# Thirteen experts sorted by load, none fixed at the end, and one light list treated apart in the ending

## The chip, the cores and the metric

The kernel runs on one core of one Trainium2 chip. A core has a matmul engine (PE, with its weight loads PEld), a vector engine (DVE), an activation engine (ACT), a general engine (POOL), a sync engine (SP) that only issues transfers here, and 16 DMA engines. The metric is the device time of one execution in microseconds (us); less is better. A profile is one further execution, recorded by the hardware profiler.

## The reference, cut to what matters

One block of a network over 512 tokens of width 1024: a token mixer, and after it a mixture of 16 experts in which every token goes to 2 experts. Only the second half is touched by the change.

```
h2 = modulate(rmsnorm(x, g_pre_ffn), shift2, scale2)
x = x + gate2 * rmsnorm(hier_moe(h2), g_post_ffn)

hier_moe: g_sel = argmax(h @ w_router_group); top 2 of the 4 experts of that group
  for e in range(16):
    a = silu(h @ w_gate[e]) * (h @ w_up[e])          # 1024 -> 512
    y = y + combine[:, e, None] * (a @ w_down[e])    # 512 -> 1024
```

All is float32. The weights of one expert are 3 x 2 MB, those of all experts 96 MB; they are read once from HBM.

## The kernel before, in words

**Lists.** After the router the kernel makes, for each expert, a list of the tokens that chose it, in slots of 128, 64 or 32 rows. Positions are numbered by `c`. Three experts are static (`c` 0 to 2, 128 slots). Eleven (`NDYN`, `c` 3 to 13) are sorted by load on the chip, heaviest first: the first `NHV` = 5 ranks have 128 slots, the next `NL64` = 3 have 64, the last three 32. The weights of a sorted expert are loaded from an address in a register of SP. Two more experts (`c` 14 and 15) are fixed, with 128 slots each. `c` = 16 (`NE`) is an extra list of 32 slots for the tokens of the heaviest expert beyond 128. If any list is longer than its slots, a loop at the end (`tc.If(novf > 0)`) does the rest with a second pass over the output.

**Positions.** `SEQ` gives the order in which the experts are worked off, one `position` each: `gate_up` (eight blocks of 512 KB, gate and up in turn, four parts of two) and `down` (four blocks of 512 KB), `down` one position late. A list of 128 slots is heavy: ACT and DVE split each weight block into a high and a low part (lines 1328 and 1329), and PE makes three products. A list of 64 or 32 slots is light: PE takes the blocks as they are (tiles `gul` and `yl`), in 2 or 4 groups of rows. The blocks go through a ring of 25 buffers in SBUF; SP issues the loads in program order (line 1306).

**Output.** `down` scales its product by the router's weight (ACT, line 1556 for a light list, 1559 and 1560 for a heavy one), and POOL adds the rows to `ybuf` in HBM by an indirect transfer (line 1580). The rows of `h2` are fetched by POOL as well (line 1335).

**Ending.** `setup` runs in the last position: SP loads the last blocks early, then a broadcast row `g2` and the rows `x1` (lines 1825, 1829), and POOL loads the four tiles `ys` of `ybuf` (line 1832). `scale` takes each tile's norm: a square sum on ACT (1845), a small operation on DVE (1840), a power on POOL (1841), a product on DVE (1847), and a product with `rest` on POOL (1850), the share of the tile's tokens that the ending does not treat apart. `write` makes the output tile on DVE (1854) and SP stores it (1855). `after(engine, ...)` chains an instruction behind the last one of its engine. The two fixed experts are treated apart: their rows are gathered from `ybuf` before their product is in it (1815), `last` adds the product and takes the norm per row, `put` scales them, and an indirect transfer adds them to the output (1872), one expert after the other.

**Small numbers for the routing.** `R(...)` takes columns of a small buffer; `ohr` is the one-hot matrix of the sort (`NDYN` x `NDYN`), and `rest` is made from `Ab`, which says who chose which expert. `psA` is a pool of four PSUM banks, from which the output projection before the experts takes its tiles `y`: four for its left half, then again four for its right half (line 1221 and following, helpers `wout_mm`, `half`).

Of the kernel before, what the change touches and what calls it, by code (L numbers as in the profile page):

```python
# [21 lines left out]
EPS = 1e-6  # L22
# [3 lines left out]
NE, DE = 16, 512  # L26
NOV = 13

NPRE, NDYN = 3, 11

NHV, NL64 = 5, 3
STAR = NPRE

SEQ = [0, 1, 2, 11, 3, 8, 4, 12, 5, 9, 6, 13, 7, 10, 14, 15]


def groups_of(c):

    r = c - NPRE
    return 4 if c == NE else 1 if r < NHV or r >= NDYN else 2 if r < NHV + NL64 else 4  # L40

def expert_at(p):

    return 4 * (p % 4) + p // 4

NA1, NA2, LOW, NRAW, NHL = 10, 5, 100, 25, 5
# [130 lines left out]
def body(ctx, tc, I, C, out, dbg=None):  # L179
# [1236 lines left out]
    def indices(x0_, x1_, src):  # L1416
        return V.scalar_tensor_tensor(iiv[:, x0_:x1_], src[:, :, 0], OOB, src[:, :, 1], op0=OP.add, op1=OP.add)
# [231 lines left out]
    with tc.issue_after(listed.ins):  # L1649
# [4 lines left out]
        ohr, t3 = R(NDYN, NDYN), R(NDYN, 3, NDYN)  # L1654
# [41 lines left out]
        indices(NPRE + NDYN, NE, ls[:, NPRE + NDYN:NE, :])  # L1696
        for c in range(NPRE + NDYN, NE):
            lsr[c] = ls[:, c, :]

        NLT = NDYN - NHV  # L1700
        lst2, ix = R(NLT + 1, 3), R(NLT + 1)
# [44 lines left out]
    parts_sum(l4v[:, 1:4, :, 1], lqv[:, :, 32:80].rearrange("p q (e c) -> p q e c", c=3))  # L1746
    G.tensor_scalar(l4v[:, :, :, 0].bitcast(I32), lof, OOB, None, op0=OP.add)

    rest = R(4)
    V.tensor_tensor(rest, Ab[:, :, NE - 2], Ab[:, :, NE - 1], op=OP.add)  # L1750
    V.tensor_scalar(rest, rest, -1.0, 1.0, op0=OP.mult, op1=OP.add)
    run["upto"] = len(seq)
    for e in range(1, NPRE):
        position(e, static_w(e))
# [103 lines left out]
    def last(i):  # L1858
        yg, w, c = fin["yg"][i], lists_of(LAST[i])[1], 24 + 4 * i
        for n in range(2):  # L1860
            s = slice(n * 512, n * 512 + 512)
            after(V, lambda: V.scalar_tensor_tensor(yg[:, s], py[i][n], w, yg[:, s], op0=OP.mult, op1=OP.add))
            after(S, lambda: S.activation(fin["junk"][:, s], yg[:, s], AF.Square, accum_out=st[:, c + 3 * n:c + 3 * n + 1]))
        after(V, lambda: V.tensor_tensor(st[:, c:c + 1], st[:, c:c + 1], st[:, c + 3:c + 4], op=OP.add))
        inv(c)
        after(V, lambda: V.tensor_tensor(yg.ap, yg.ap, fin["G2"], op=OP.mult))

    def put(i):
        zg, r = fin["yg"][i], st[:, 25 + 4 * i:26 + 4 * i]
        after(S, lambda: S.mul(zg[:, 0:512], zg[:, 0:512], r))  # L1870
        after(V, lambda: V.tensor_scalar(zg[:, 512:1024], zg[:, 512:1024], r, None, op0=OP.mult))
        after(G, lambda: G.indirect_dma_start(out=outv, out_offset=bass.IndirectOffsetOnAxis(ap=iiv[:, LAST[i]:LAST[i] + 1], axis=0),
                                              in_=zg.ap, in_offset=None, bounds_check=T - 1, oob_is_err=False, compute_op=OP.add))


    def last_products(raws):
        sg = run["pend"][2][0][0]
        tp = pT("at")
        for q in range(4):
            PE.transpose(tp[:, q * 128:(q + 1) * 128], sg[:, q * 128:(q + 1) * 128], ident)  # L1880
        after(S, lambda: S.copy(sg.ap, tp))
        y = pA("y0"), pA("y1")
        for kk in range(4):
            for n in range(2):
                mm(y[n], sg[:, kk * 128:kk * 128 + 128], raws[kk][:, n * 512:n * 512 + 512], kk == 0, kk == 3)
        py.append(y)

    py = []

    def first():  # L1890
        py.append(run["py"])
        for tt in range(2):
            scale(tt, True)

    run.update(setup=lambda: setup(True), first=first)
    for n in range(NPRE, NE):
        c = SEQ[n]
        if c >= NPRE + NDYN:
            position(n, static_w(c))
        else:  # L1900
            position(n, dyn_w(nc.values_load(idi[0:1, c:c + 1], engines=(mybir.EngineType.SP,), min_val=0, max_val=NE - 1)))
    raws = [raw_unit(run["pend"][1], 2, kk) for kk in range(4)]
    line.update({V: run["mul"], S: run["silu"]})
# [9 lines left out]
    for i in range(2):  # L1913
        for n in range(2):
            s = slice(n * 512, n * 512 + 512)
            after(S, lambda: S.mul(yob[i][:, s], py[i][n], lists_of(LAST[i])[1]))
# [47 lines left out]
```

## Time and profile before

| | |
|---|---|
| Runs shown | 640.63, 642.20, 642.83 us; median 642.2 |
| Profiled execution | 641.7 us, of which 639.9 us is the span from first to last instruction |
| PE, DVE, ACT, POOL busy | 86%, 58%, 46%, 34% of the span |
| PE clock granted, mean | 0.949 of 2.4 GHz |
| DMA, mean | 265 GB/s, 169.43 MB |

The span is what the rows below tell of; 1.8 us lie around it. A share of busy time is a mean over stages with different limits, so each claim is read from its own stage.

### The profile page before, as it was taken

To read this page: it belongs to the slowest core of one execution; us is meant where nothing else is said; L and a number is where in the kernel's file an instruction comes from. 1 tells how busy PE (TensorE), PEld (TensorE's weight loads), DVE (VectorE), ACT (ScalarE), POOL (GpSimd) and SP (SyncE) were. 2 spreads that over 40 slices of the span, in tenths; PEclk is the share of its full clock that TensorE was granted. 3 is DMA by queue.
4 is the path that set the end of the run, shared out by engine and by line. 5 is a ranking of instruction groups with operands and counts; after the bars stand their busy time and mean duration, and the time that the engine had idled before them with its cause. 6 is when DMAs were issued, how large, how long until landed. Compare 5 with 4: busy or idle time off the path is not lost.

```text
span 639.9 us, 9115 instructions
## 1 busy us (share of the span) xinstructions
PE 548.7 (86%) x3065; PEld 379.3 (59%) x3065; DVE 368.1 (58%) x689; ACT 294.5 (46%) x478; POOL 218.4 (34%) x264
## 2 busy tenths in 40 slices
PE   3779979699999869998679899999999989988940
PEld 1256955688665547875568676657654647355610
DVE  3560693826237663427978997753653527165781
ACT  2560626443125335224258684653744545165722
POOL 8343850066124345617440317312211010002152
PEclk9979998899999988999599999999999999999985
DMA  9975601121599794247689799999999999999631
GB/s 266 389 257 190 239 0 33 50 82 66 174 321 311 263 352 165 67 163 270 239 340 357 254 350 398 335 369 381 387 383 391 384 387 390 390 404 372 263 134 24
DMA packets 59542, 169.43 MB, mean 265 GB/s; under 512 B 9433, under 2 KB 16885, under 8 KB 59492
## 3 DMA queue, kind: packets, MB, share of 16 engines
q1 hardware_dynamic: 50820, 156.17, 65.4%
q0 software_dynamic: 6112, 12.18, 7.4%
q10 hardware_dynamic: 2560, 0.47, 0.5%
q8 instruction: 25, 0.41, 0.3%
q14 instruction: 25, 0.20, 0.1%
HBM read 157.02 MB, written 17.12 MB: 272 GB/s over the span
## 4 chain that ended last, share of the span: by engine, by line
PE 52%; DMA 19%; DVE 12%; issue 6%; POOL 6%; ACT 4%; POOLq 0%; ACTq 0%; DVEq 0%; SPq 0%
PE y L211 9%; DMA U<-in_w_gate_dram 9%; PE gate L211 6%; PE up L211 6%; PE gul L211 4%; PE uz L211 3%; DMA U<-in_w_ada_dram 3%; PE yl L211 2%; PE win L211 2%; PE ada2p L839 2%; PE num L211 2%; DMA U<-in_w_down_dram 2%; PE xe L211 1%; DVE U L489 1%; PE ada1p L211 1%
## 5 line engine op out<-in xcount | busy, mean ns | idle before, releaser
L1329 DVE TENSOR_TENSOR U<-U,U 128x1024 fp32r<-128x1024 f32 x114 | 135.5, 1232 | 42.7 <-ACT U L1328 42.2
L1328 ACT CAST U<-U 128x1024 fp32r<-128x1024 f32 x114 | 114.1, 1051 | 17.9 <-PE pos L211 7.0
L211 PE MATMUL y<-U,U 128*128 128x512 f32 x364 | 99.2, 413 | 3.4 <-ACT U L1328 1.9
L211 PEld LDWEIGHTS y<-U,U 128*128 128x128 f32 x364 | 67.8, 192 | 23.0 <-issue 3.6
L211 PE MATMUL gate<-U,U 128*128 128x512 f32 x186 | 55.4, 401 | 2.5 <-DVE U L1329 1.9
L211 PE MATMUL up<-U,U 128*128 128x512 f32 x188 | 55.8, 397 | 1.6 <-ACT U L1328 1.4
L211 PE MATMUL uz<-U,U 128*128 128x512 f32 x192 | 52.6, 409 | 0.3 <-ACT U L602 0.2
L214 POOL TENSOR_TENSOR U<-U,U 128x512 fp32r<-128x512 f32 (+2 forms) x32 | 43.1, 1363 | 4.1 <-ACT U L811 1.5
L211 PEld LDWEIGHTS uz<-U,U 128*128 128x128 f32 x192 | 34.9, 189 | 12.3 <-issue 5.5
L211 PEld LDWEIGHTS up<-U,U 128*128 128x128 f32 x188 | 35.0, 189 | 11.1 <-ACT U L1328 2.5
L211 PEld LDWEIGHTS gate<-U,U 128*128 128x128 f32 x186 | 34.2, 189 | 12.4 <-DVE U L1329 3.2
L211 PE MATMUL gul<-U,U 128*32 128x256 f32 (+1 forms) x312 | 40.0, 444 | 0.0
L1580 POOL DMA_INDIRECT ybuf<-U x8 | 14.3, 1782 | 66.4 <-ACT U L1556 50.9
L1580 POOL DMA_INDIRECT ybuf<-U,U x7 | 11.0, 1576 | 73.3 <-ACT U L1560 54.9
L1335 POOL DMA_INDIRECT U<-h2d,U x16 | 18.5, 1158 | 35.5 <-DVE U L1692 20.2
L211 PE MATMUL win<-U,U 128*128 128x512 f32 x96 | 26.1, 419 | 0.0
L1366 DVE TENSOR_TENSOR U<-xet,U 128x512 fp32r<-128x512 f32 x18 | 12.1, 686 | 21.9 <-ACT U L1365 21.9
L211 PE MATMUL gate<-U 128*128 128x512 f32 x54 | 20.9, 422 | 3.2 <-ACT U L1328 1.7
L214 DVE TENSOR_TENSOR U<-U,U 128x512 fp32r<-128x512 f32 (+1 forms) x18 | 15.9, 906 | 12.9 <-PE crow L211 9.2
L211 PEld LDWEIGHTS gul<-U,U 128*32 128x32 f32 (+1 forms) x312 | 13.9, 117 | 15.2 <-issue 9.6
L426 ACT CAST U<-U 128x512 fp32r<-128x512 f32 (+2 forms) x30 | 21.1, 763 | 3.4 <-DMA U<-in_w_in_dram 3.4
L211 PEld LDWEIGHTS win<-U,U 128*128 128x128 f32 x96 | 18.2, 199 | 6.7 <-issue 2.5
(446 smaller groups left out, 1032.9 us busy)
## 6 DMA issues: line engine op xcount, KB each, us to landing
U<-in_w_gate_dram SPq DMA_DIRECT2D x64, 512.0 KB
U<-in_w_up_dram SPq DMA_DIRECT2D x64, 512.0 KB
U<-in_w_down_dram SPq DMA_DIRECT2D x64, 512.0 KB
U<-in_w_ada_dram SPq DMA_DIRECT2D x48, 512.0 KB
U<-in_w_in_dram SPq DMA_DIRECT2D x6, 1024.0 KB
U<-in_w_out_dram SPq DMA_DIRECT2D x4, 1024.0 KB
U<-in_x_dram SPq DMA_DIRECT2D x4, 512.0 KB
x0d<-U SPq DMA_DIRECT2D x4, 512.0 KB
```

The costliest lines, as they stand in the source:

```text
L211: PE.matmul(out=o, lhsT=l, rhs=r, start=start, stop=stop)
L214: (eng or V).tensor_tensor(o, a, b, op=OP.subtract)
L426: S.copy(hi[:, s], raw[:, s])
L489: V.scalar_tensor_tensor(ca[:, o:o + L], xx[:, m, 0:L], w[0], ca[:, o:o + L], op0=OP.mult, op1=OP.add)
L839: return PE.matmul(out=ps[32 * j:32 * j + 32, :], lhsT=cst[:, k, :], rhs=rs[j // 2][:, 512 * (j % 2):512 * (j % 2) + 512], start=k == 0, s ...
L1328: after(S, lambda: S.copy(hi.ap, r.ap))
L1329: after(V, lambda: V.tensor_tensor(lo.ap, r.ap, hi.ap.bitcast(F32), op=OP.subtract))
L1335: g = G.indirect_dma_start(out=xe[0:n], out_offset=None, in_=h2d[:, :], in_offset=bass.IndirectOffsetOnAxis(ap=gi[0:n], axis=0), bounds_ch ...
L1366: V.tensor_tensor(xl[:, s], tp, xh[:, s].bitcast(F32), op=OP.subtract)
L1580: run["scatter"] = G.indirect_dma_start(out=to, out_offset=bass.IndirectOffsetOnAxis(ap=gi, axis=0), in_=yo[:, 0:n], in_offset=None, bound ...
```

## The change

Thirteen experts are sorted instead of eleven, six of them with 128 slots; none is fixed at the end. `SEQ` changes so that the last position is the least loaded expert with 32 slots, and the one before it has 64. All positions from the fourth on take their weights by register. The ending treats only the last list apart: its rows lie in four groups of 32, each with a quarter of the columns, so one gather, one add, one square of 256 columns and one indirect store do. Their square sums are added over the four groups by a matmul with a constant `f4`, which POOL builds from the identity in 16 small operations. `rest` is picked by the one-hot row of the last rank.

```
-NPRE, NDYN = 3, 11
-NHV, NL64 = 5, 3
+NPRE, NDYN = 3, 13
+NHV, NL64 = 6, 3
-SEQ = [0, 1, 2, 11, 3, 8, 4, 12, 5, 9, 6, 13, 7, 10, 14, 15]
+SEQ = [0, 1, 2, 12, 3, 9, 4, 13, 5, 10, 6, 14, 7, 8, 11, 15]
...
         if n == NE - 1:
-            mid[1] = lambda: run.update(py=down(pend, box["ya"], keep=True))
-            mid[2:] = [run["setup"], run["first"]]
+            mid[1:] = [lambda: down(pend, box["ya"]), run["setup"]]
...
-    rest = R(4)
-    V.tensor_tensor(rest, Ab[:, :, NE - 2], Ab[:, :, NE - 1], op=OP.add)
+    rest, tl = R(4), R(4, NDYN)
+    V.tensor_tensor(tl, Ab[:, :, D_], bc(ohr[:, NDYN - 1:NDYN, :], [128, 4, NDYN]), op=OP.mult)
+    V.tensor_reduce(rest, tl, axis=AX.X, op=OP.add)
     V.tensor_scalar(rest, rest, -1.0, 1.0, op0=OP.mult, op1=OP.add)
+    f4 = R(128)
+    for j in range(4):
+        G.tensor_copy(f4[:, 32 * j:32 * j + 32], ident[:, 0:32])
+        for i in range(1, 4):
+            G.tensor_tensor(f4[:, 32 * j:32 * j + 32], f4[:, 32 * j:32 * j + 32], ident[:, 32 * i:32 * i + 32], op=OP.add)
...
         eng = G if part else SP
+        if part:
+            lb = next_raw()
+            fin.update(yg=lb[:, 0:LC], G2p=lb[:, LC:2 * LC], lj=lb[:, 2 * LC:3 * LC])
+            for j in range(lg_):
+                m = 128 // lg_
+                SP.dma_start(out=fin["G2p"][j * m:j * m + m], in_=bc(g2d[:, j * LC:j * LC + LC], [m, LC]))
+            line[G] = G.indirect_dma_start(out=fin["yg"], ..., in_=parts(ybuf[:, :]), ...)
         for tt in range(4):
             line[eng] = eng.dma_start(out=fin["ys"][tt].ap, in_=ybuf[tt * 128:(tt + 1) * 128, :])
-        if part:
-            fin.update(yg=[next_raw() for _ in LAST])
-            for yg, p in zip(fin["yg"], LAST):
-                after(G, lambda: gather(yg.ap, ybuf, iiv[:, p:p + 1], T))
...
-    last_products(raws)
+    py = down(run["pend"], keep=True)[0][:, 0:LC]
+    yg, lj = fin["yg"], fin["lj"]
+    sq_, tot = st[:, 24:25], psX.tile([128, 512], F32, name="tot", tag="X")
+    after(V, lambda: V.scalar_tensor_tensor(yg, py, lw2, yg, op0=OP.mult, op1=OP.add))
+    after(S, lambda: S.activation(lj, yg, AF.Square, accum_out=sq_))
+    mm(tot[:, 0:1], f4, sq_, True, True)
+    after(V, lambda: V.tensor_tensor(yg, yg, fin["G2p"], op=OP.mult))
+    after(V, lambda: V.tensor_scalar(st[:, 26:27], tot[:, 0:1], 1.0 / D, EPS, op0=OP.mult, op1=OP.add))
+    after(G, lambda: G.tensor_tensor(st[:, 25:26], st[:, 26:27], mhalf[:, 0:1], op=OP.pow))
+    for tt in range(2):
+        scale(tt, True)
+    after(V, lambda: V.tensor_scalar(yg, yg, st[:, 25:26], None, op0=OP.mult))
+    write(0)
     for tt in range(2, 4):
         scale(tt, True)
-    for tt in range(4):
-        write(tt)
-    last(0)
-    put(0)
-    last(1)
-    put(1)
+        write(tt - 1)
+    write(3)
+    after(G, lambda: G.indirect_dma_start(out=parts(outv), ..., in_=yg, ..., compute_op=OP.add))
```

Lines move by one up to 1627 or so and by a few behind that: 1328 before is 1327 after. Three places show how the instructions stand.

POOL, just ahead of the last four low parts of the output projection's weights (`TENSOR_TENSOR U_1846<-U_992,U_1857`), before:

```order
L214 TENSOR_TENSOR U_1867<-U_99,U_1867 128x512
L1058 COPY U_99<-U_81 128x8
L1061 MEMSET U_99 128x1 x8
L214 TENSOR_TENSOR U_1846<-U_992,U_1857 128x512 x4
L1773 MEMSET U_2007 128x16
```

The same place after:

```order
L213 TENSOR_TENSOR U_1867<-U_99,U_1867 128x512
L1057 COPY U_99<-U_81 128x8
L1060 MEMSET U_99 128x1 x8
L1751 COPY U_99<-U_81 128x32 x4
L1753 TENSOR_TENSOR U_99<-U_99,U_81 128x32 x12
L213 TENSOR_TENSOR U_1846<-U_992,U_1857 128x512 x4
L1190 TENSOR_TENSOR U_75<-U_75 128x1
```

The 16 operations that build `f4` now stand ahead of the four low parts.

POOL around the loads from `ybuf` in the last position (scatters into `ybuf`, then loads from it), before:

```order
L1580 DMA ybuf<-U_2431,U_99 512x1024
L1580 DMA ybuf<-U_99 1024x512
L1832 DMA U_2431<-ybuf 128x1024
L1832 DMA U_2426<-ybuf 128x1024
L1832 DMA U_103<-ybuf 128x1024
L1832 DMA U_81<-ybuf 128x1024
L1815 DMA U_2431<-ybuf,U_99 128x1024
L1815 DMA U_75<-ybuf,U_99 128x1024
```

And after:

```order
L1579 DMA ybuf<-U_99 512x1024
L1579 DMA ybuf<-U_2431,U_99 1024x512
L1838 DMA U_2431<-ybuf,U_99 128x256
L1841 DMA U_2431<-ybuf 128x1024
L1841 DMA U_2426<-ybuf 128x1024
L1841 DMA U_103<-ybuf 128x1024
L1841 DMA U_81<-ybuf 128x1024
L1878 TENSOR_TENSOR U_75<-U_75 128x1
```

The last scatter ahead of the loads is now that of the next to last position (the 64-slot list); it was that of the position before that one. The one small gather stands ahead of the four tiles.

PE at its end, before (the turn of a tile `at` and the first products of the last fixed expert's `down` that follow it):

```order
L211 MATMUL up<-U_2006,U_2430 128x512
L1880 MATMUL at<-U_81,U_1832 128x128 x4
L211 MATMUL y_4605<-U_2432,U_1832 128x512
L211 MATMUL y_4606<-U_2432,U_1832 128x512
L211 MATMUL y_4605<-U_2007,U_1832 128x512
L211 MATMUL y_4606<-U_2007,U_1832 128x512
```

And after, from the `down` of the next to last position (`yl`, 64 rows) to the end:

```order
L210 MATMUL yl<-U_2007,U_1832 64x512 x2
L210 MATMUL yl<-U_99,U_1832 64x512 x2
L210 MATMUL yl<-U_2426,U_1832 64x512 x2
L210 MATMUL yl<-U_99,U_1832 64x512 x2
L210 MATMUL gul<-U_2432,U_2007 32x256 x8
L1500 MATMUL at<-U_81,U_1832 128x128 x2
L210 MATMUL yl<-U_2432,U_1832 32x256 x4
L210 MATMUL yl<-U_2007,U_1832 32x256 x4
L210 MATMUL tot<-U_75,U_99 128x1
```

The last two positions need no split blocks any more.

## Rows read from the trace of the kernel before

**Rows 1.** The page's DMA rate in 40 slices of 16 us.

```profile
GB/s 266 389 257 190 239 0 33 50 82 66 174 321 311 263 352 165 67 163 270 239 340 357 254 350 398 335 369 381 387 383 391 384 387 390 390 404 372 263 134 24
```

**Rows 2.** The chain that ended last, from 555 us on: start, length, what.

```profile
558.69 9.88 DMA U<-in_w_gate_dram
...
604.44 1.37 PE up L211 x6
...
624.15 6.36 DMA out_dram<-U,U
```

**Rows 3.** The timeline of SP's transfers in the last positions: start, length, line, what. The four blocks of `down` of the next to last and of the last position, the four `x1`.

```profile
566.23 4.11 SPq L1306 DMA_DIRECT2D U<-in_w_down_dram  x4
...
578.81 4.10 SPq L1306 DMA_DIRECT2D U<-in_w_down_dram  x4
585.12 4.73 SPq L1829 DMA_DIRECT2D U<-x1d  x4
```

**Rows 4.** What SP's queue waited for, first from 326 to 440 us, then from 480 to 600 us: us in total, times, longest.

```profile
SPq L1306 <- DVE U L1329: 29.0, 20, 7.3
...
SPq L1306 <- DMA U<-in_w_down_dram: 23.8, 28, 3.1
```

**Rows 5.** The timeline from the `down` of the last light list to the loads from `ybuf`; in brackets the idle time before and what ended it.

```profile
576.63 3.65 PE L211 MATMUL yl<-U,U 128*64 128x512 f32 x14
...
580.32 0.69 ACT L1556 ACTIVATE U<-yl,U 128x512 f32<-128x512 f32 x1 [7.99 <-PE yl L211]
...
581.28 1.54 POOL L1580 DMA_INDIRECT ybuf<-U  x1 [9.96 <-ACT U L1556]
...
589.49 2.25 POOL L1832 DMA_DIRECT2D U<-ybuf  x4 [6.68 <-DVE U L1490]
...
592.04 1.08 POOL L1815 DMA_INDIRECT U<-ybuf,U  x1 [0.30 <-DMA U<-x1d]
```

**Rows 6.** Time from issue to landing in three lines, in this order: the four `ys` tiles (1832), the scatters into `ybuf` (1580), the indirect stores to the output (1872).

```profile
DMA to landing us min/median/max: 6.8/10.1/13.5
...
DMA to landing us min/median/max: 7.0/8.9/10.5
...
DMA to landing us min/median/max: 4.7/5.6/6.4
```

**Rows 7.** Busy time in four stretches: stretch, its length, busy us (and instructions) of PE, PEld, DVE, ACT, POOL, then the granted PE clock, the DMA share and GB/s.

```profile
234.00:235.00 1.00, 0.00 (x0) 0.00 (x0) 0.00 (x0) 0.00 (x0) 0.92 (x2) 1.00 1.00 393
...
237.00:238.00 1.00, 0.18 (x1) 0.18 (x1) 1.00 (x2) 0.00 (x0) 1.00 (x2) 0.50 1.03 410
...
602.00:603.00 1.00, 1.00 (x6) 0.83 (x5) 0.81 (x2) 0.00 (x0) 0.11 (x1) 1.00 0.45 184
...
621.00:622.00 1.00, 0.00 (x0) 0.00 (x0) 0.96 (x3) 0.00 (x0) 0.66 (x1) 0.50 0.07 25
```

**Rows 8.** The timeline of the ending.

```profile
602.89 0.58 POOL L1841 TENSOR_TENSOR U<-U 128x1 f32<-128x1 f32 x1 [8.35 <-DVE U L1840]
603.55 0.19 POOL L1850 TENSOR_TENSOR U<-U,U 128x1 f32<-128x1 f32 x1
...
609.01 1.06 ACT L1845 ACTIVATE U<-U 128x1024 f32<-128x1024 f32 x1
609.98 0.19 ACT L1845 ACTIVATION_READ_ACCUMULATOR U<-U 128x1 f32 x1
...
612.65 1.60 POOL L1841 TENSOR_TENSOR U<-U 128x1 f32<-128x1 f32 x1
614.33 0.76 POOL L1850 TENSOR_TENSOR U<-U,U 128x1 f32<-128x1 f32 x1
...
617.51 1.28 DVE L1854 SCALAR_TENSOR_TENSOR U<-U,U,U 128x1024 f32<-128x1024 f32 x1
631.33 1.60 POOL L1872 DMA_INDIRECT out_dram<-U,U  x1 [3.94 <-ACTq L1920]
```

**Rows 9.** The timeline around the place of the 16 small operations on POOL, and one POOL operation on 64 columns from a stretch in which DVE was busy.

```profile
261.13 0.18 POOL L1058 COPY U<-U 128x8 f32<-128x8 f32 x1
261.56 5.03 POOL L214 TENSOR_TENSOR U<-U,U 128x512 fp32r<-128x512 f32 x4
266.62 1.14 ACT L1324 CAST U<-U 128x512 fp32r<-128x512 f32 x2 [9.24 <-POOL U L214]
268.48 2.03 DVE L1157 TENSOR_TENSOR U<-y,U 128x512 f32<-128x512 f32 x3
271.68 0.60 ACT L1156 ACTIVATE U<-y 128x512 f32<-128x512 f32 x1 [1.90 <-PE y L211]
...
385.14 1.21 POOL L1781 TENSOR_TENSOR U<-U 128x64 f32<-128x64 f32 x1 [3.10 <-DVE U L1780]
```

**Rows 10.** The timeline of DVE in the routing, three operations on the one-hot matrix (121 and 3 x 121 numbers), and the chain where PE takes up its work behind it.

```profile
339.01 0.27 DVE L1667 TENSOR_TENSOR U<-U,U 128x121 f32<-128x121 f32 x1
...
357.33 0.68 DVE L1688 TENSOR_TENSOR U<-U 128x363 f32<-128x363 f32 x1
...
358.60 0.53 DVE L1690 TENSOR_REDUCE U<-U 128x33 f32<-128x363 f32 x1
...
367.97 1.67 PE gate L211 x6
```

**Rows 11.** The costliest groups of instructions, DVE's half of the split of heavy weight blocks: busy us and mean ns of one, then the idle time ahead and what ended it.

```profile
L1329 DVE TENSOR_TENSOR U<-U,U 128x1024 fp32r<-128x1024 f32 x114 | 135.5, 1232 | 42.7 <-ACT U L1328 42.2
```

More of the change, by code (lines that the diff above doesn't have):

```diff
@@ L27 @@
 NOV = 13
-NPRE, NDYN = 3, 11
-NHV, NL64 = 5, 3
+NPRE, NDYN = 3, 13
+NHV, NL64 = 6, 3
 STAR = NPRE
-SEQ = [0, 1, 2, 11, 3, 8, 4, 12, 5, 9, 6, 13, 7, 10, 14, 15]
+SEQ = [0, 1, 2, 12, 3, 9, 4, 13, 5, 10, 6, 14, 7, 8, 11, 15]
 def groups_of(c):
     r = c - NPRE
-    return 4 if c == NE else 1 if r < NHV or r >= NDYN else 2 if r < NHV + NL64 else 4
+    return 4 if c == NE else 1 if r < NHV else 2 if r < NHV + NL64 else 4
 def expert_at(p):
@@ L1653, in body @@
         cnt, key, rank = R(16), R(NDYN), R(NDYN)
-        ohr, t3 = R(NDYN, NDYN), R(NDYN, 3, NDYN)
+        ohr, t3 = R(NDYN, NDYN), xtb[:, 0:3 * NDYN * NDYN].rearrange("p (r c e) -> p r c e", r=NDYN, c=3)
         over, idf, cntr, lsd = R(NDYN), R(16), R(NDYN), R(NDYN, 3)
@@ L1695, in body @@
             lsr[NPRE + r] = lsd[:, r, :]
-        indices(NPRE + NDYN, NE, ls[:, NPRE + NDYN:NE, :])
-        for c in range(NPRE + NDYN, NE):
-            lsr[c] = ls[:, c, :]
         NLT = NDYN - NHV
@@ L1807, in dyn_w @@
         return src
-    LAST = NE - 2, NE - 1
     outv = out.rearrange("o t c -> (o t) c")
     fin = {}
-    def gather(dst, src, idx, rows):
-        return G.indirect_dma_start(out=dst, out_offset=None, in_=src[:, :], in_offset=bass.IndirectOffsetOnAxis(ap=idx, axis=0),
-                                    bounds_check=rows - 1, oob_is_err=False)
+    lg_, li, lw2 = groups_of(NE - 1), lists_of(NE - 1)[2], lists_of(NE - 1)[3]
+    LC = D // lg_
+    parts = lambda a: a.rearrange("t (h c) -> (t h) c", c=LC)
     def setup(part):
+        wsrc = run.get("wsrc")
         if part:
             for kind, q in ((0, 3), (1, 3), (2, 0), (2, 1), (2, 2), (2, 3)):
-                early[kind, q] = load(static_w(NE - 1), kind, q)
+                early[kind, q] = load(wsrc, kind, q)
                 rawb.pop()
@@ L1830, in setup @@
         eng = G if part else SP
+        if part:
[4 more added lines that the diff above has]
+                SP.dma_start(out=fin["G2p"][j * m:j * m + m], in_=bc(g2d[:, j * LC:j * LC + LC], [m, LC]))
+            line[G] = G.indirect_dma_start(out=fin["yg"], out_offset=None, in_=parts(ybuf[:, :]), in_offset=bass.IndirectOffsetOnAxis(ap=li, axis=0),
+                                           bounds_check=T * lg_ - 1, oob_is_err=False)
         for tt in range(4):
             line[eng] = eng.dma_start(out=fin["ys"][tt].ap, in_=ybuf[tt * 128:(tt + 1) * 128, :])
-        if part:
-            fin.update(yg=[next_raw() for _ in LAST])
-            for yg, p in zip(fin["yg"], LAST):
-                after(G, lambda: gather(yg.ap, ybuf, iiv[:, p:p + 1], T))
     def inv(c):
@@ L1855, in write @@
         after(SP, lambda: SP.dma_start(out=outv[tt * 128:(tt + 1) * 128, :], in_=y2))
[L1858 to L1873, printed above, removed]
@@ L1876, in last_products @@
[L1876 to L1893, printed above, removed]
@@ L1895, in body @@
-    run.update(setup=lambda: setup(True), first=first)
+    run.update(setup=lambda: setup(True))
     for n in range(NPRE, NE):
         c = SEQ[n]
[L1898 to L1903, printed above, removed]
-    last_products(raws)
+        run["wsrc"] = dyn_w(nc.values_load(idi[0:1, c:c + 1], engines=(mybir.EngineType.SP,), min_val=0, max_val=NE - 1))
+        position(n, run["wsrc"])
@@ new lines, in body @@
+    line.pop(V, None)
+    line.pop(S, None)
+    py = down(run["pend"], keep=True)[0][:, 0:LC]
[6 more added lines that the diff above has]
+    after(V, lambda: V.tensor_scalar(st[:, 26:27], tot[:, 0:1], 1.0 / D, EPS, op0=OP.mult, op1=OP.add))
@@ L1905, in body @@
+    after(G, lambda: G.tensor_tensor(st[:, 25:26], st[:, 26:27], mhalf[:, 0:1], op=OP.pow))
[3 more added lines that the diff above has]
+    write(0)
     for tt in range(2, 4):
         scale(tt, True)
-    for tt in range(4):
-        write(tt)
-    last(0)
-    put(0)
-    last(1)
-    put(1)
[L1913 to L1916, printed above, removed]
+        write(tt - 1)
@@ L1919, in body @@
+    write(3)
+    after(G, lambda: G.indirect_dma_start(out=parts(outv), out_offset=bass.IndirectOffsetOnAxis(ap=li, axis=0), in_=yg, in_offset=None,
+                                          bounds_check=T * lg_ - 1, oob_is_err=False, compute_op=OP.add))
+    after(S, lambda: S.mul(yob[0][:, 0:LC], py, lw2))
     novf = nc.values_load(exiv[0:1, 28:29], min_val=0, max_val=NOV)
     with tc.If(novf > 0):
-        for i, p in enumerate(LAST):
-            scatter(yob[i], iiv[:, p:p + 1])
+        scatter(yob[0], li, LC)
```

## The prediction

> **What bounds the kernel now.** I read the page's rate in slices first. From 480 us on the weights come at some 390 GB/s in every slice until 576 us; after that the rate falls away [rows 1]. The chain of waits says the same: near 560 us it is made of weight transfers of some 10 us each, and later of matmuls (at 604.44 PE works without a wait on `up`), until the indirect store of the output [rows 2]. So the kernel ends in three stages: a stream of weights that is the bound, two heavy positions whose products PE still owes when the stream has gone by, and the ending.
>
> The waits of SP's queue show what holds the stream. From 480 us on SP waits for landings of loads before. From 326 to 440 us it waits for buffers that DVE's split frees, 29.0 us in 20 waits [rows 4]. The stream there runs below its later rate. I take from this that a delay of PE or DVE before 440 us is passed on whole to the end of the stream.
>
> **The change part by part.** Up to the 13th position the order of kinds (128, 64, 32 slots) is the same as before, so only the routing, `f4` and the last three positions count.
>
> *One heavy position fewer.* Twelve blocks are no longer split; on DVE that is 12 x 1.23 = 14.8 us [rows 11]. While the stream is the bound this buys nothing; it counts only behind the stream, where I work the ending out anew, from the landing of the last weights of the next to last position.
>
> *Landing.* SP issues the four `down` loads of the last position from 578.81 to 582.9, each when the load it waits for, a `down` of the next to last position issued from 566.23, has landed [rows 3]. I put the last landing at 582.6. The bytes in front of it are the same after the change.
>
> *Next to last position, 64 slots.* `yl` takes 3.65 us for four blocks [rows 5], 0.9 for the block that comes last. PE has little to do there, and after an idle stretch its granted clock was 0.50 (237 to 238 us, idle three us before) [rows 7]; so 1.8 us: 584.4. POOL's scatter starts 0.96 behind the start of ACT's scaling (581.28 - 580.32) [rows 5]: 585.4. From that scatter to the first load of `ys` it was 8.2 us (589.49 - 581.28) [rows 5], the landing of the scatter, whose issue to landing is 7.0 to 10.5 [rows 6]: 593.6. The new small gather stands ahead, 1.08 + 0.30 [rows 5]: the first `ys` is issued at 595.0.
>
> *The four tiles.* The last landing took 13.5 us at most [rows 6]; behind the first issue that is at best 13.5, at worst 15.2 with the 1.7 us of three issues. When the queue was alone, at 602 to 603 us, it moved 184 GB/s [rows 7]; 2 MB at that rate are 11.4 us, so other traffic was not what made them slow. I take 13.5: 608.5. Then a square sum on ACT of 1.06 + 0.19 [rows 8]: 609.8, a small operation on DVE, 0.2: 610.0, on POOL 1.60 + 0.76 [rows 8]: 612.4 (0.58 + 0.19 is the other bound, from a stretch with little on DVE, 1.6 us sooner [rows 8]). The other way in gives the same: the first tile lands 6.8 after 595.0, its square takes 1.25, and four times 2.36 on POOL end at 612.5. One product on DVE, 1.28 [rows 8]: 613.7.
>
> *Last store.* The output tile must land before the indirect store may start. Before, the last product ended at 618.8, at 621 nothing much moved any more (share 0.07), and the indirect store started at 624.15: between 2.2 and 5.4 us [rows 2, 7, 8]. I take 3.5, plus 0.4 for issues and rounding: 617.6. Before, the second indirect store started at 631.33 and the span ended at 639.9, 8.6 behind [rows 8]: **626.2**. The first one had to land (6.36 on the chain [rows 2]) before the second; that wait is gone, as there is one list.
>
> *`f4` on POOL.* Twelve sums and four copies of 32 columns stand ahead of the last four low parts, which POOL makes back to back (261.56 for 5.03). ACT's cast behind them had already waited 9.24 us for POOL and starts at 266.62, and DVE's product that frees PE's banks follows at 268.48, its first of three ends near 269.1 [rows 9]. PE needs the bank near 271.6, since ACT reads its product from 271.68 [rows 9]; so PE has 2.5 us in hand. A sum of 32 columns lies between a 128 x 1 (0.19 [rows 8]) and a 128 x 512 (5.03 / 4 = 1.26 [rows 9]), on the line between 0.25, and 0.08 to the next (603.55 - 603.47) [rows 8]: 12 x 0.33 + 4 x 0.2 (copy 0.18 [rows 9]) = 4.8 us. PE loses 4.8 - 2.5 = **2.3 us**. Queued behind the low parts are all casts and products of that half.
>
> *Routing on DVE.* Matrices of 11 x 11 become 13 x 13. From 0.27 for 121 numbers and 0.68 or 0.53 for 363 [rows 10] a number costs 1.1 to 1.7 ns; 48 more are 0.05 to 0.08, in seven operations; 144 more are 0.15 to 0.24, in two. With one operation more (0.2) and one less (0.16) that is 0.7 to 1.1. DVE is busy without a break there, and PE takes up its work at 367.97 behind it [rows 10]: I take **0.7 us**.
>
> *At nothing:* loads by register on SP, which waits for landings anyway [rows 4]; if not, 0.3 us per issue at most; the last list's own branch (its gather lands first, and its add, square, matmul and power come to some 3 us while the `ys` land); the new `rest`, made while the weights stream.
>
> Sum: 626.2 + 2.3 + 0.7 = 629.2 for the span; with the 1.8 us around it **631.0 us**, against 641.7 of the profiled execution, which stands 0.5 below the median of the runs.
>
> **The rivals.**
> B, `f4` hidden: the sums are as short as 0.19 and PE's slack is larger. Then 628.7 us. Against it: DVE is idle there and POOL is not.
>
> F, the tiles land sooner. The shortest transfer of POOL's queue took 4.7 us [rows 6]. With that for the first tile, and the others close behind, POOL's four steps set the end: 595.0 + 4.7 + 1.25 + 9.4 + 1.3 = 611.7, 2.0 us less, 629.0. For it: less other traffic than before. Against it: the 184 GB/s of the queue alone. The Trainium skill, "DMA: Bandwidth & Descriptors", section "Anatomy of one DMA — SWDGE (gpsimd) path", gives 2.0 us and the bytes over 436 GB/s for such a transfer, an estimate of 3.2 us for 512 KB; by it the sum would be 627.5. The trace does not agree: 6.8 to 13.5 us for each of four that run together.
>
> C, a later tail: the scatter takes its longest, 10.5 instead of 8.2 (+2.3), and the tiles 15.2 instead of 13.5 (+1.7) [rows 6]: 635.0. For it: two scatters now follow each other closely, and the gather lies ahead of the tiles.
>
> D, the other side: POOL's small sums cost 1.21 each, as one on 64 columns did where DVE was busy [rows 9]. Sixteen are 19.4 us; less the 2.5 in hand PE stalls 16.9 instead of 2.3, all passed on: 645.6, slower. It decides from some 0.95 us per operation on, where the 10.7 us of gain are spent. Against it: DVE is idle at 261 us.
>
> E, the change does not do what it says: a list is longer than its slots and the loop at the end runs. Each of its 12 loads takes at least 1.3 us at 390 GB/s [rows 1], and the output is read and written again; it ends beyond 650. Against it: the reference's router on the drawn inputs gives the 13 sorted experts 137, 111, 95, 88, 74, 68, then 64, 60, 37, then 29, 26, 25, 23 tokens; all fit, the 9 beyond 128 in the extra list.
>
> **How the numbers follow.** The main sum gets 0.55, B 0.08, F 0.12, C 0.20, D 0.04, E 0.01. B and F differ from the sum by 2 to 3.5 us, C by 4. The range reaches to F's lower end and a little below B, and beyond C by its half: 626.5 to 636.5; outside are D, E and the tails of the others. A difference of 0.3%, 1.9 us, is about what a measurement of this kernel can tell from no change. All of A, B, F and nearly all of C lie more than that below 642.2: faster 0.92, same 0.03, slower 0.05.
>
> **What would show it.** In the changed kernel: POOL's sums near 261.5 and their length (0.25); the start of ACT's cast, 4.8 later than 266.62, and a gap of PE near 271.6 of some 2 us; PE's `gate` behind the routing 3 us later than 367.97; the same rate from 480 us on; the last weights of the next to last position near 585.6; the granted clock at the last 64-slot `yl` (0.50); the first `ys` issued near 598.0 and the last landed near 611.5; the last product's end near 616.7, one indirect store near 620.6, the span's end at 629.2. The prediction is wrong if POOL's sums are longer than 0.6 us each, if the stream ends later than the shift, if the scatter or the tiles land later than their longest before, or if a loop runs.

## The result, and the profile after

The changed kernel took 634.51 us (median of 4 runs, 632.71 to 636.78), the kernel before 641.79 (4 runs): ratio 0.9889, interval 0.9847 to 0.9931. Two further comparisons gave 0.9923 (0.9893 to 0.9952) and 0.9902 (0.9875 to 0.9929); the median of all 16 runs of the changed kernel is 635.05. The three medians lie 4.7 to 7.3 us below those of the kernel before; the forecast was 10.7. The profiled execution of the changed kernel has a span of 635.0 us.

First, the stretch in which the last weights come, before from 445 to 580 us and after from 445 to 590: length, busy us (and instructions) of PE, PEld, DVE, ACT, POOL, then the granted clock, DMA share and GB/s.

```profile
445.00:580.00 135.00, 124.69 (x663) 74.04 (x661) 64.34 (x66) 63.40 (x84) 19.16 (x15) 0.99 1.03 389
```

```profile
445.00:590.00 145.00, 136.66 (x716) 86.12 (x714) 73.10 (x73) 72.99 (x96) 22.34 (x16) 0.99 1.03 384
```

Both limits are there at once: the queues are full (share 1.03) and PE is busy 92% and 94% of the time. What PE waited for after, from 445 to 597 us (us in total, times, longest), tells which of them was the later one. The two longest of nine lines:

```profile
PE gate L210 <- ACT U L1327: 2.2, 3, 1.5
PE at L1500 <- ACT U L1486: 1.9, 3, 0.7
```

No landing of a weight stands in any of the nine, and SP still waits almost only for landings all the while, as it did in [rows 4]. A queue that waits for landings shows that the queue is full, not that anybody waits for what it brings.

The timeline of the last positions and the ending, after (start, length, engine, line, what; in brackets the idle time before):

```profile
585.95 4.13 SPq L1305 DMA_DIRECT2D U<-in_w_down_dram  x4
587.23 1.54 POOL L1579 DMA_INDIRECT ybuf<-U  x1 [9.12 <-ACT U L1559]
592.59 3.65 PE L210 MATMUL yl<-U,U 128*64 128x512 f32 x16
596.30 0.69 ACT L1555 ACTIVATE U<-yl,U 128x512 f32<-128x512 f32 x1 [5.02 <-PE yl L210]
597.26 1.54 POOL L1579 DMA_INDIRECT ybuf<-U,U  x1 [8.48 <-ACT U L1555]
605.84 1.08 POOL L1838 DMA_INDIRECT U<-ybuf,U  x1 [7.04 <-DMA U<-g2d]
606.92 2.23 POOL L1841 DMA_DIRECT2D U<-ybuf  x4
611.45 1.04 ACT L1850 ACTIVATE U<-U 128x1024 f32<-128x1024 f32 x1
621.52 1.28 DVE L1859 SCALAR_TENSOR_TENSOR U<-U,U,U 128x1024 f32<-128x1024 f32 x1
626.64 1.71 POOL L1887 DMA_INDIRECT out_dram<-U,U  x1 [5.15 <-SPq L1893]
```

These answer to [rows 3], [rows 5] and [rows 8]. The first row is the issue of the last `down` loads; when the last of them goes out, at some 589.8, the last weights of the position before have landed. The 64-row products begin only at 592.59 and run without a break at a granted clock of 1.00, 16 in 3.65 us: PE was behind its weights and had no need to wait for them. The scatter of their rows had a second limit close by: the one before it, issued at 587.23, landed 8.9 us later, at 596.1, and the rows themselves were ready at 597.0 (596.30 + 0.69). The four tiles, issue to landing:

```profile
DMA to landing us min/median/max: 4.5/5.7/6.9
```

Before it was 6.8 to 13.5 [rows 6].

All profiles, counted from the issue of their first expert weight load, since what lies ahead of it drifts (that issue stood at 224.9 to 234.6 us, though nothing ahead of it was changed). In us: issue of the 10th load; the 40th to the 46th; the 97th to the 142nd; issue of the 189th; last scatter; first `ys` tile issued; end of the last output tile's product on DVE; end of the span.

| | 10th | 40-46 | 97-142 | 189th | scatter | tile | product | end |
|---|---|---|---|---|---|---|---|---|
| before | 57.1 | 17.1 | 69.0 | 350.7 | 353.1 | 361.4 | 390.7 | 411.7 |
| before, again | 56.3 | 17.1 | 69.6 | 350.3 | 351.9 | 360.6 | 389.4 | 410.4 |
| after | 57.9 | 19.2 | 71.4 | 355.7 | 367.0 | 376.7 | 392.6 | 404.8 |
| after, again | 58.4 | 19.2 | 71.5 | 356.8 | 367.9 | 377.6 | 393.6 | 405.8 |
| after, third | 58.6 | 19.0 | 71.2 | 356.8 | 368.4 | 378.2 | 393.9 | 406.0 |
| light_between | 58.6 | 19.0 | 71.3 | 355.8 | 367.9 | 377.4 | 392.6 | 404.8 |
| lights_last | 57.5 | 19.1 | 70.7 | 355.9 | 366.7 | 376.6 | 392.2 | 404.4 |
| four_lights_last | 57.9 | 19.2 | 71.7 | 357.5 | 362.7 | 372.0 | 394.5 | 406.7 |
| f4_three_times | 66.5 | 19.0 | 71.3 | 364.9 | 376.5 | 386.0 | 401.9 | 414.1 |
| f4_elsewhere | 57.7 | 21.2 | 70.5 | 353.9 | 368.1 | 377.5 | 393.6 | 405.8 |
| warm_routing | 58.2 | 17.8 | 71.3 | 354.9 | 364.7 | 374.3 | 392.0 | 404.2 |
| gather_last | 57.8 | 19.2 | 71.2 | 355.5 | 366.5 | 374.9 | 393.3 | 406.3 |
| between_warm_f4 | 57.2 | 20.0 | 71.0 | 356.9 | 367.6 | 377.2 | 393.8 | 406.0 |
| lights_warm_f4 | 56.6 | 20.3 | 70.5 | 355.0 | 368.0 | 377.7 | 394.2 | 406.4 |

By this count the prediction's end was 629.2 - 228.1 = 401.1; the three profiles of the changed kernel end 3.7 to 4.9 later.

The last two columns show where the gain lies. From the last output tile's product to the end it was 21.0 us before, with the two indirect stores one behind the other, and is 12.2 now. The product itself comes 1.9 to 4.5 us later than before, and 4.4 to 6.9 us are left.

### The profile page after: what moved, and what is told of

It reads as the page before. It is cut to its first block, busy times and chain, and to the rows that moved or that the text cites. A ratio compares the mean times of both kernels' runs of the same rounds, so it can differ in the third digit from the quotient of the medians.

```text
span 635.0 us, 9192 instructions
## 1 busy us (share of the span) xinstructions
PE 537.8 (85%) x3097; PEld 370.3 (58%) x3097; DVE 352.9 (56%) x671; ACT 281.4 (44%) x460; POOL 218.8 (34%) x278
## 5 line engine op out<-in xcount | busy, mean ns | idle before, releaser
L1328 DVE TENSOR_TENSOR U<-U,U 128x1024 fp32r<-128x1024 f32 x106 | 126.6, 1234 | 33.0 <-ACT U L1327 32.3
L1327 ACT CAST U<-U 128x1024 fp32r<-128x1024 f32 x106 | 107.1, 1051 | 18.1 <-PE pos L210 6.6
L210 PE MATMUL y<-U,U 128*128 128x512 f32 x352 | 93.2, 404 | 1.6 <-POOL U L213 0.6
L210 PEld LDWEIGHTS y<-U,U 128*128 128x128 f32 x352 | 64.8, 190 | 19.3 <-issue 2.0
L210 PE MATMUL gate<-U,U 128*128 128x512 f32 x166 | 50.2, 408 | 2.8 <-ACT U L1327 2.2
L210 PE MATMUL up<-U,U 128*128 128x512 f32 x164 | 49.7, 400 | 1.5 <-DVE U L1328 0.8
L210 PE MATMUL gul<-U,U 128*32 128x256 f32 (+1 forms) x368 | 44.7, 435 | 0.0
L210 PEld LDWEIGHTS up<-U,U 128*128 128x128 f32 x164 | 30.9, 192 | 10.0 <-DVE U L1328 1.6
L210 PEld LDWEIGHTS gul<-U,U 128*32 128x32 f32 (+1 forms) x368 | 16.1, 116 | 18.5 <-issue 10.7
L1334 POOL DMA_INDIRECT U<-h2d,U x16 | 19.2, 1201 | 13.7 <-PE xlt L1346 5.5
L210 PE MATMUL yl<-U,U 128*32 128x256 f32 (+1 forms) x180 | 21.5, 438 | 0.7 <-DVE U L1505 0.7
L210 PEld LDWEIGHTS num<-U,U 128*128 128x128 f32 x128 | 17.4, 191 | 4.7 <-DVE U L920 1.7
```

The costliest lines, as they stand in the source:

```text
L210: PE.matmul(out=o, lhsT=l, rhs=r, start=start, stop=stop)
L1327: after(S, lambda: S.copy(hi.ap, r.ap))
L1328: after(V, lambda: V.tensor_tensor(lo.ap, r.ap, hi.ap.bitcast(F32), op=OP.subtract))
L1334: g = G.indirect_dma_start(out=xe[0:n], out_offset=None, in_=h2d[:, :], in_offset=bass.IndirectOffsetOnAxis(ap=gi[0:n], axis=0), bounds_ch ...
```

## The experiments

All are edits of the changed kernel unless said otherwise. Each was compared with the kernel before on the same chip; the ratios are to that kernel. The changed kernel stood at 0.9889 in the first comparison. Light_between, lights_last and f4_three_times ran beside it on one chip (0.9923), f4_elsewhere and the two versions of the last experiment on another (0.9902). For four_lights_last, warm_routing and gather_last it did not run on the same chip, so that only the ratios and the table tell how they stand to it.

**Second and third profiles.** No edit.

> The changed kernel once more, for a second profile beside the first. Theory: in the first profile the changed kernel was already 2.0 us behind the kernel before at 228 us, where nothing had been changed yet; that is drift from one execution to the next and will not stand here in the same size, so the span lies 1 to 3 us below the 635.0 of the first profile. The rest of the shift stays: some 0.5 us at the 16 small sums, some 2 us in the routing, and the 64-row products of the next to last position end 5 us behind the landing of their weights. Rival: the 2.0 us belong to the change (a buffer placed elsewhere) and stand here again.

> The changed kernel a third time, so that the three below stand beside it on one chip. 4 to 7 us below the kernel before, as in the two comparisons so far.

> The kernel before once more, for a second profile. In five profiles of the changed kernel and its variants the stretch from the 97th to the 142nd weight load took 70.7 to 71.5 us, in the one profile of the kernel before 69.0. If the 2.3 us are of the change, this profile shows 68.5 to 69.5 again; if they are drift, 70 or more. The routing stretch (40th to 46th load) shows 17.1 again (19.0 to 19.2 in the five).

636.06 us against 640.80, and 634.55 against 640.01; the kernel before again 639.8 (one run). The 2.0 us by which the first profile was late at 228 us did not come again: drift. The routing's 2.0 us stood in every profile that left it alone (19.0 to 19.2 against 17.1), and the 97th to the 142nd load took 69.0 and 69.6 before, 70.5 to 71.7 in all twelve others.

**Where PE's lag comes from.**

```
-SEQ = [0, 1, 2, 12, 3, 9, 4, 13, 5, 10, 6, 14, 7, 8, 11, 15]
+SEQ = [0, 1, 2, 12, 3, 9, 4, 13, 5, 10, 6, 7, 14, 8, 11, 15]    light_between
+SEQ = [0, 1, 2, 12, 3, 9, 4, 13, 5, 6, 10, 7, 8, 14, 11, 15]    lights_last
+SEQ = [0, 1, 2, 12, 3, 9, 4, 5, 10, 6, 7, 8, 13, 11, 14, 15]    four_lights_last
```

> A 32-slot position stands between the last two heavy ones instead of ahead of both. Theory: in the changed kernel PE still owes products of two heavy positions in a row when the weights of the 64-slot list have landed, so that its 64-row products end some 5 us behind the landing; with a light position between, they end 1 to 2 us behind it and the kernel is 2 to 4.5 us faster than the changed one. Rival: the products are late because their weights land late; then no change. Second rival: they are earlier, but the four tiles that are loaded after them land more slowly, since they meet the last other loads; then 0 to 2 us faster.

> The last three positions are light (32, 64, 32 slots), and the heavy ones move ahead by one place each from the tenth on. Theory of PE's lag: the 64-row products follow the landing of their weights within 1.5 us and the kernel is 3 to 5 us faster than the changed one. Rival: more heavy positions in a row earlier hold up the release of weight buffers, the stream ends later, and the gain is spent (0 to 3 us slower).

> The last four positions are light (32, 64, 32, 32 slots), the heavy ones move ahead. With three light ones at the end PE was no longer late, but the scatters followed each other at 8 to 10 us, each behind the landing of the one before, and that chain set the loads of the tiles. Theory: with the last heavy scatter some 16 us earlier the chain has room, the last scatter goes out with the last products, and the first tile is issued 2 to 3 us earlier than there: 3 to 6 us faster than the changed kernel. Rival: heavy positions in a row hold up weight buffers before 440 us, and the stream ends as much later.

633.13 (0.9883, 0.9850 to 0.9916), 633.73 (0.9890, 0.9853 to 0.9926) and 638.97 (0.9951, 0.9925 to 0.9976). The first two medians are 2.9 and 2.3 us below the changed kernel's 636.06 on that chip. The intervals of the ratios overlap with its own, though, and by the table the two profiles end at 404.8 and 404.4, where the changed kernel ended at 404.8 to 406.0. Whether they gain a us or two stays open.

The theory that two heavy positions in a row make the lag fell. With a light one between them the last scatter stood where it was, at 367.9, and the 64-row products ended 7.2 us behind the issue of the last `down` load, where it was 6.3 to 6.8 in the changed kernel. With three light positions at the end it was 2.4. What counts, I read from this, is how much light work stands behind the last heavy products.

In lights_last the 64-row products ended at 589.53, 2.5 to 3.9 us earlier by the table's count, but their scatter did not follow them. The timeline of lights_last:

```profile
584.94 1.56 POOL L1579 DMA_INDIRECT ybuf<-U  x1 [8.35 <-ACT U L1504]
585.88 3.65 PE L210 MATMUL yl<-U,U 128*64 128x512 f32 x16
589.58 0.69 ACT L1555 ACTIVATE U<-yl,U 128x512 f32<-128x512 f32 x1 [5.02 <-PE yl L210]
592.72 1.56 POOL L1579 DMA_INDIRECT ybuf<-U,U  x1 [6.22 <-DMA U<-in_w_down_dram]
601.54 1.07 POOL L1838 DMA_INDIRECT U<-ybuf,U  x1 [7.26 <-DMA U<-g2d]
```

The rows were ready at 590.3; the scatter waited till 592.72, 7.8 us behind the one before it, and the gather 8.8 us behind that. Scatters into `ybuf` wait for the landing of the scatter before (here 584.94 landed at 592.0; the row names a weight load, but what POOL waited for up to 592.0 was the semaphore of that scatter), so at the end they are a chain of their own. In the changed kernel that chain stood 0.8 to 0.9 us behind PE in all three profiles. So earlier 64-row products alone could not have brought the last scatter forward by more than that.

With four light positions at the end the picture that I had predicted for these products came at last, though not the 3 to 6 us expected of it: the kernel was no faster than the changed one. PE in four_lights_last:

```profile
592.08 0.64 PE L210 MATMUL yl<-U,U 128*32 128x256 f32 x8 [0.32 <-DMA U<-in_w_down_dram]
593.25 0.64 PE L210 MATMUL yl<-U,U 128*32 128x256 f32 x8 [0.54 <-DMA U<-in_w_down_dram]
594.53 0.64 PE L210 MATMUL yl<-U,U 128*32 128x256 f32 x8 [0.64 <-DMA U<-in_w_down_dram]
595.85 0.64 PE L210 MATMUL yl<-U,U 128*32 128x256 f32 x8 [0.68 <-DMA U<-in_w_down_dram]
```

The last block costs 0.64 behind its landing; the last scatter is 4.3 to 5.7 us earlier in the table, and the tiles' loads 4.7 to 6.2. Yet the last product is 0.6 to 1.9 later. Its tiles met other loads (SP's queue moved 1.0 MB in the 7 us behind the issue of the first tile, 0.1 in the changed kernel) and took longer. Then DVE stood behind the row of `g2` for the last list, of which SP had issued the last part only at 608. The tiles from issue to landing, and DVE's wait:

```profile
DMA to landing us min/median/max: 7.3/9.5/10.7
```

```profile
618.02 0.43 DVE L1876 TENSOR_TENSOR U<-U 128x256 f32<-128x256 f32 x1 [6.23 <-DMA U<-g2d]
```

So here the branch that I had put at nothing holds up everything: the program puts the tiles' arithmetic on DVE behind that product. The 189th load is 0.7 to 1.8 later than in the changed kernel as well, which is the way of the rival, but too little to be all of it.

**What a delay on POOL and a stop of PE cost.**

```
-    for j in range(4):
+    for j in 3 * list(range(4)):                                  f4_three_times
-        G.tensor_copy(f4[...], ident[:, 0:32])
+        G.tensor_tensor(f4[...], ident[:, 0:32], bc(cnt[:, 0:1], [128, 32]), op=OP.pow)    f4_elsewhere
```

> The 16 small operations on POOL are made three times over (same result). In the changed kernel they took 3.0 us and PE lost some 0.5 of it, which would be a slack of 2.4 us. Theory: 6.0 us more on POOL, all of it past the slack, PE is 6.0 us later, and nothing gives it back: the last weights land 6 us later and the kernel is 5 to 6.5 us slower than the changed one. Rival: the weight buffers take it up before the stream becomes the bound: 0 to 2 us slower.

> The first four of the 16 small operations raise the identity to the power of a token count (same values), so that POOL can make them only after the lists, at some 340 us, where it waits for DVE. Theory: PE's loss ahead of the first ten weight loads (57.5 to 58.6 us from the first load to the tenth, against 56.3 and 57.1 in the kernel before) goes back to 56.3 to 57.1, and the kernel is 0.5 to 1.5 us faster than the changed one. Rival: the loss there is drift, no change; or POOL is late in the routing and the stretch from the 40th to the 46th load grows from 19.2.

f4_three_times took 642.19 (1.0020, 0.9995 to 1.0044), 6.1 more than the changed kernel in the same comparison. PE's wait at this place grew from 0.60 to 6.50 us, nearly the 6.0 that POOL had more; that much of the theory holds. In the changed kernel and in f4_three_times:

```profile
274.17 1.20 PE L210 MATMUL y<-U,U 128*128 128x512 f32 x4 [0.60 <-DVE U L1156]
```

```profile
276.16 14.04 PE L210 MATMUL y<-U,U 128*128 128x512 f32 x48 [6.50 <-DVE U L1156]
```

By the table, though, the 10th load is 7.9 to 8.6 later and the end 8.1 to 9.3. The stop also cost the clock, which fell to 0.50 (1.2 of 2.4 GHz), in the windows of f4_three_times (columns as above):

```profile
272.00:277.00 5.00, 0.84 (x2) 0.75 (x3) 2.76 (x5) 3.34 (x9) 1.53 (x2) 0.50 0.11 16
277.00:282.00 5.00, 5.00 (x13) 3.83 (x13) 2.35 (x4) 1.59 (x4) 0.00 (x0) 0.50 0.99 395
282.00:287.00 5.00, 5.00 (x23) 4.09 (x22) 0.09 (x1) 0.00 (x0) 0.00 (x0) 0.97 0.35 113
```

PE did 13 matmuls in the second window at 0.50 and 23 in the third, nearly all of it at full clock. None of the delay was given back later.

f4_elsewhere took 636.21 (0.9928, 0.9906 to 0.9951): no gain. Its time does not tell what `f4` costs in its first place, since four powers of 32 columns hold POOL for 22.8 us, and the gathers of rows behind them come late, with a routing of 21.2 instead of 19.2:

```profile
333.81 22.82 POOL L1751 TENSOR_TENSOR U<-U,U 128x32 f32<-128x32 f32 x4 [1.56 <-DVE U L1659]
```

Its profile does tell it. PE does not wait at all where it waited 0.60 us in the three profiles of the changed kernel. The 10th load came at 57.7, and at 57.2 and 56.6 in the two versions further down that move `f4` as well; in the eight profiles with `f4` in its first place it came at 57.5 to 58.6. On average that is 0.9 earlier. So `f4` cost some 0.6 to 0.9 us there. And the 189th load was issued 2 to 3 us earlier than in the changed kernel, but the last scatter was not earlier: 368.1. What came with the weights earlier, PE could not use.

**The routing's clock.**

```
         G.tensor_scalar(rk2[:, q, :], rk, 128.0 * (q + 1), None, op0=OP.subtract)
+        if q == 1:
+            for _ in range(5):
+                mm(lq[:, 256:512], ident, k1[:, 0:256], True, True)
```

> Five idle products of 256 columns fill PE's empty 2 us in the routing (their result is not read). Theory: in the changed kernel PE stands still there for 2.07 us, the granted clock falls to 0.50 for 6.8 us, and half of the routing's extra 2.0 us comes from that; with the products the clock stays at 1.00, the stretch from the 40th to the 46th weight load falls from 19.2 to 17.8 to 18.4 us, and the kernel is 0.8 to 1.5 us faster than the changed one. Rival: DVE, not PE, sets the pace there; the clock stays up and the stretch stays at 19.2.

633.69 (0.9887, 0.9857 to 0.9917). In the kernel before, PE stood still for 0.88 us ahead of a product of `lq`, and the granted clock stayed at 1.00:

```profile
362.48 0.46 PE L211 MATMUL lq<-U,U 128*128 128x80 bf16 x8 [0.88 <-DVE U L1070]
```

```profile
363.00:365.00 2.00, 2.00 (x13) 1.78 (x14) 2.00 (x4) 0.95 (x2) 1.36 (x2) 1.00 0.71 242
```

In the changed kernel it stands still for 2.07 us there, the granted clock falls to 0.50, and DVE later waits for PE:

```profile
364.73 0.38 PE L210 MATMUL lq<-U,U 128*128 128x80 bf16 x4 [2.07 <-DVE U L1069]
```

```profile
365.00:367.00 2.00, 2.00 (x23) 1.77 (x22) 2.00 (x4) 0.17 (x1) 0.57 (x1) 0.50 0.38 55
367.00:369.00 2.00, 2.00 (x5) 1.54 (x6) 1.67 (x4) 1.15 (x2) 1.63 (x2) 0.50 0.94 365
```

```profile
370.25 0.26 DVE L1645 TENSOR_REDUCE U<-lq 128x48 f32<-128x96 f32 x1 [1.58 <-PE lq L210]
```

With the idle products the same place in warm_routing:

```profile
358.15 1.99 PE L210 MATMUL lq<-U 128*128 128x256 f32 x8 [0.61 <-DVE U L1645]
```

```profile
360.00:362.00 2.00, 2.00 (x24) 1.66 (x24) 1.75 (x4) 0.89 (x1) 0.67 (x2) 1.00 0.32 61
362.00:364.00 2.00, 2.00 (x17) 1.49 (x17) 2.00 (x7) 0.16 (x1) 1.37 (x1) 1.00 0.99 403
```

The clock stays up and the stretch falls from 19.2 to 17.8, as the theory said. The last scatter is 2.3 to 3.7 earlier than in the changed kernel, but the end only 0.6 to 1.8: the tiles, now nearer to the other loads (0.35 MB by SP's queue in the 7 us behind the first issue, not 0.1), took 6.2 to 8.3 us instead of 4.5 to 6.9.

**The gather behind the tiles.**

```
-            line[G] = G.indirect_dma_start(out=fin["yg"], ...)
         for tt in range(4):
             line[eng] = eng.dma_start(out=fin["ys"][tt].ap, ...)
+        if part:
+            line[G] = G.indirect_dma_start(out=fin["yg"], ...)
...                                  (its arithmetic behind scale(3) and write(2))
```

> The gather of the last list's rows is issued behind the four tiles, not ahead of them, and its arithmetic is moved behind that of the tiles. Theory: the first tile is issued 8.4 to 8.8 us behind the scatter, not 9.7, and everything behind it is 1.1 us earlier; with one power less in POOL's chain up to 1.7 us. Rival: the small branch is late now and holds up the last store: 0 or slower.

635.22 (0.9919, 0.9886 to 0.9952): nothing gained. The first tile went out 8.4 behind the scatter, not 9.7, as expected; but the tiles took 5.9 to 7.9, and two operations of the last list now stood on DVE ahead of the last output tile. In gather_last:

```profile
617.54 0.48 DVE L1880 SCALAR_TENSOR_TENSOR U<-yl,U,U 128x256 f32<-128x256 f32 x1
618.60 0.43 DVE L1883 TENSOR_TENSOR U<-U 128x256 f32<-128x256 f32 x1 [0.57 <-ACT U L1881]
618.94 1.28 DVE L1860 SCALAR_TENSOR_TENSOR U<-U,U,U 128x1024 f32<-128x1024 f32 x1
```

The rival was right.

**Together.** The order of light_between, or of lights_last, with the idle products and the later `f4`.

> The light position between the last two heavy ones, the five idle products in the routing, and the 16 small operations behind the lists, all three. If their effects add (2.9, 2.3 and 1.0 us by the runs so far): 5 to 6 us faster than the changed kernel; if the first two medians were mostly drift (the profiles, counted from the first weight load, showed 1.0 and 1.6): 2.5 to 4 us faster.

> The same with the last three positions light. By the profiles counted from the first weight load (1.4 for the order, 1.4 for the clock, 1.0 for the sums): 3 to 4 us faster than the changed kernel. Rival: what comes earlier meets the last weight loads, the tiles land more slowly, and the gain is under 2 us.

634.94 (0.9895, 0.9865 to 0.9925) and 635.23 (0.9919, 0.9896 to 0.9942). The gains that both expected did not come: the changed kernel took 634.55 there. Only the rival of the second, under 2 us, allowed for that. The four powers were still in them, with a routing of 20.0 and 20.3; the order and the idle products together without the powers were not run. No version is shown to be better than the changed kernel; for light_between, lights_last and warm_routing it stays open.

## Why the prediction was right, and where it was wrong

The direction was right, and for the reason given: one store at the end where two had followed each other (21.0 us from the last product to the end, now 12.2). The likeliest value was 3.5 us too low, and the gain 0.4 to 0.7 of what was forecast. That the time lies within the range is in part luck: a scatter 7 us late and tiles 3 us quicker than forecast took something from each other, and the upper end had been set for a rival that did not occur. How much of the gain is due to the heavy position fewer and how much to the one store, no run here separates. Point by point, in the table's count:

- **Landing.** Predicted shift of the stream 3.0; the 189th load was 5.0 to 6.5 later than in the two profiles before. Of that, `f4`: predicted 2.3, measured 0.6 to 0.9, by PE's wait and by the 10th load with `f4` moved. The 16 operations took 3.0 us (2.42 for twelve sums, 0.65 for four copies), not 4.8, since a sum took 0.20 and not 0.33; the 2.5 us that PE had in hand were right (3.0 less 0.60). That is nearly **rival B**, which got 0.08. The 10th load was 0.8 to 2.3 later than before; what `f4` does not explain of that is open. Routing: predicted 0.7, measured 1.9 to 2.1. The wider operations are there (0.88 and 0.67 us instead of 0.68 and 0.53 in [rows 10]), but the step left out that the later hand-over lets PE stand still for 2.07 us instead of 0.88, that the clock then falls to 0.50, and that DVE in turn waits for PE; warm_routing gives back 1.2 to 1.4 of it. The remaining 1.6 to 2.5 are the stretch from the 97th to the 142nd load.
- **"`yl` takes 0.9 for the block that comes last. PE has little to do there."** This step failed. The predicted last scatter was 585.4 + 3.0 - 228.1 = 360.3; measured 367.0 to 368.4. Reading [rows 2] and [rows 4] I took the full queues for the bound of everything and PE for a follower. But PE was 92% busy there before, too, and it was late: the weights of the 64-row products of [rows 5] had been asked for from 550.58 us on, the fourth at 554.34, and the eighth load behind that one was issued at 564.99, by when they had landed; the products began at 574.48, 10 us later, and the rest of them ran from 576.63 on without a break. One heavy position fewer took some 10 us of products away (twelve blocks of 1.37 [rows 2] are 16.4; a 32-slot position takes about 6, twice 2.05 of `gul` and 1.9 of `yl`) and so made PE's debt smaller, it did not pay it: in the row of 592.59 above, the products end 6.5 us behind the issue of 589.8. Two rows of SP in the timeline of before, beside PE's row of [rows 5], would have told me:

```profile
550.58 4.09 SPq L1306 DMA_DIRECT2D U<-in_w_down_dram  x4
564.99 0.61 SPq L1306 DMA_DIRECT2D U<-in_w_up_dram  x1
```

  Four_lights_last shows what the step would have needed, more light positions behind the last heavy one; f4_elsewhere shows that earlier weights alone do not help. The step also left out the scatter before, which had to land first and did so only 0.8 to 0.9 us before the rows were ready.
- **Scatter to first tile.** Predicted 9.6, measured 9.7 to 9.8.
- **The clock at `yl`.** Predicted 0.50, measured 1.00 (592.59 to 596.24 us): PE had not been idle.
- **The tiles.** Predicted 13.5 to the last landing; a tile took 4.5 to 6.9, and first issue to last product was 15.6 to 16.0 instead of 18.7. Rival F's mechanism came true, since next to nothing else was in the queues by then (0.1 MB in 7 us, where SP's queue had moved 2.0 in the same stretch of the kernel before). The argument against it, 184 GB/s for "the queue alone" [rows 7], was wrong: the third of the four tiles had landed at 602.2, so that row is the tail of the transfers, and from 610 to 612 us of the changed kernel the four tiles moved at 373 GB/s. By the Trainium skill ("DMA: Bandwidth & Descriptors", "Anatomy of one DMA — SWDGE (gpsimd) path") a tile by itself would take 3.2 us as an estimate. No run here has a tile by itself; the first of four took 3.8 to 4.6 where little else was in the queues.
- **Last store and end.** Last product to end 12.5 predicted, 12.2 measured in all three profiles.
- **Rival C** named 635.0, nearly the time measured, for a cause that did not occur: the scatter landed 7.7 us after its issue and the tiles came sooner. **D** and **E** did not occur: the sums took 0.20 each, and no loop ran.

The sum of the steps that moved: +7 at the scatter, nothing to the tile, -3 to the product, 0 to the end: some 4 us, the 3.7 to 4.9 by which the end was late.

## What to carry to other kernels

Full queues and a queue that waits for landings do not make transfers the bound; look whether a consumer ever waits for a landing, and how busy it is, before the products behind a stream are put right behind its last byte. A step that ends late by a chain of several near-equal limits gives back little for any one of them: here products, scatters that follow each other, tiles that meet other loads and a small branch took turns. And where a longer wait stops PE, as the 2.07 us did here, ask what the granted clock does next; filling the gap with idle products gave back 1.2 to 1.4 of the 2.0 us.

## What the runs showed of the hardware

A power on POOL took 5.7 us for 128 x 32 (22.82 for four, in f4_elsewhere), where a sum of that shape took 0.20. The same four tile loads from POOL's queue took 3.8 to 6.0 us each in light_between, 6.2 to 8.3 in warm_routing, where they were issued some 3 us earlier, and 7.3 to 10.7 in four_lights_last, another 2 us earlier. What made the 97th to the 142nd load 1 to 2.7 us slower in every version with 13 sorted lists, whatever their order, is open: in the three profiles of the changed kernel gathers and scatters there were as many as before, and SP waited almost only for landings.
